# Seven block products in place of eight for most of w_down, one chunk of w_up later

## The chip, the cores and the metric

The kernel runs on one core of a Trainium2 chip. Its engines work side by side, each through its own queue in order: TensorE (PE, with its weight loads as PEld), VectorE (DVE), ScalarE (ACT), GpSimd (POOL) and SyncE (SP), which issues the loads and stores. The metric is the device time of one execution in microseconds, as the median of the runs; three runs of the kernel before gave 837.82 us (836.74 to 837.98).

## What is computed

One layer of a decoder: 512 tokens of 1024 features, fp32. Two token mixers come first (a convolution and an attention), then the channel mixer that the change touches, then a gated embedding and a final norm. In the reference the channel mixer reads:

```python
hf = rmsnorm(x, norm_ffn[i])
up = causal_dwconv(hf @ w_up[i], ffn_dw_w[i], ffn_dw_b[i])
gate, val = jnp.split(up, 2, axis=-1)
x = x + (jax.nn.gelu(gate) * val) @ w_down[i]
```

`w_up` is 1024 x 5632, `w_down` 2816 x 1024, and the convolution runs over three tokens.

## The kernel before

Matrix products run in two parts: each operand is cut into a hi part (ScalarE, `hi_of`, line 107) and a lo part (VectorE, `lo_of`, line 110: the operand less its hi part), and each product takes three matmuls: hi hi, hi lo and lo hi (`mm_w`, lines 117 to 119, with weights as the stationary operand; `mm_a`, lines 123 to 125, with activations as the stationary one).

Weights come as a stream of pieces (`pieces`, class `Stream`) in their order of use. A piece is 512 KB, 128 partitions by 1024 columns. `pump` asks for loads (two raw buffers, `wraw`) and starts cuts up to four cut pieces (`whl`) ahead; `take` hands a piece to its product; `done` frees it. So a cut stands some three pieces ahead of its use in the queues of ScalarE and VectorE.

The 2816 features of the channel mixer are 22 chunks of 128. For each chunk `up_chunk` runs twice, for the gate and for the value: 24 matmuls of 512 columns into one of the eight PSUM banks (`ps`), an eviction by ScalarE (line 1170) and two taps of the convolution by VectorE (lines 1171 and 1172). Then come the gelu (line 1180), the multiplication (line 1182) and the two parts `a` of the activations. After 8, 16 and 22 chunks `rows_product` multiplies the group by its rows of `w_down`: for each column half, four row tiles of tokens, accumulated over the group's chunks in four banks and then added to x in SBUF by VectorE (`residual`, line 1137). The third group goes on into the next norm.

The order of each queue is the order in which the program is written; what is moved by hand is where `pump` and `st.work` place the stages of a cut. SyncE's queue holds every load in the order of the pieces.

Of the kernel before, what the change touches and what calls it, by code (L numbers as in the profile page):

```python
# [11 lines left out]
F32R = mybir.dt.float32r  # L12
# [29 lines left out]
# heads whose scores, two units ahead, and whose weights, one unit ahead, are due in a unit's steps  # L42
# [41 lines left out]
def block_kernel(ctx: ExitStack, tc: tile.TileContext, x, p, rel_bias, norm_mix, w_in, conv_dw_w, conv_dw_b,  # L84
# [30 lines left out]
    # out += W.T a  with W's parts as the stationary operand  # L115
# [5 lines left out]
    # out += a.T W  with the activations' parts as the stationary operand  # L121
    def mm_a(o, a_hi, a_lo, w_hi, w_lo, start, stop):
        nc.tensor.matmul(o, a_hi, w_hi, start=start, stop=False)  # L123
        nc.tensor.matmul(o, a_hi, w_lo, start=False, stop=False)  # L124
        nc.tensor.matmul(o, a_lo, w_hi, start=False, stop=stop)  # L125

# [1 line left out]
    # A piece lands as fp32 and is cut into an exact (hi, lo) pair of float32r parts, some pieces ahead of its use.  # L128
# [24 lines left out]
    CMP_AFTER = CMP_AT                      # the compression's eight pieces follow the z pieces from this one on  # L153
# [10 lines left out]
    FFN_GROUPS = ((0, 8), (8, 16), (16, NF))  # L164
    for f0, f1 in FFN_GROUPS:
# [5 lines left out]
        rows_pieces("down%d" % f0, w_down, list(range(f0, f1)))  # L171
# [4 lines left out]
    class Stream:  # L176
# [6 lines left out]
        def pump(self, force=False):  # L183
            """asks for the next pieces; starts to cut those that were asked for in an earlier call"""
            while self.stages:
                self.work()
            while self.cuts < self.dmas and (force or self.asked[self.cuts] < self.call):
                i = self.cuts
                key, _, a, b, tag = pieces[i]
                if tag is not None:  # L190
                    if tag == "whl" and self.hls >= self.limit:
                        break
                    hl = work("whl", (P, 2, a, b), F32R, tag=tag, bufs=CUT if tag == "whl" else 1)
                    self.hl[i] = hl
                    self.cut(hl, self.raw[i], a)
                    self.hls += tag == "whl"
                    self.raws -= 1
                self.cuts += 1
            while self.dmas < len(pieces):
                i = self.dmas  # L200
                key, srcs, a, b, tag = pieces[i]
                if (self.wholes if tag is None else self.raws) == 2:
# [12 lines left out]

        def cut(self, hl, raw, a):
            """in stages, so that neither engine waits for the other"""
# [28 lines left out]

        def done(self):
            self.hls -= 1
# [3 lines left out]

    st = Stream()

# [13 lines left out]
    VNG = ((0, 3), (3, 3), (6, 2))          # row blocks of the values' and branch gates' weights  # L268
# [29 lines left out]
    for _ in range(WARM):                  # keeps the tensor engine's clock up until the first rows are there  # L298
        nc.tensor.matmul(warm[:, :P], ones, grow[:, 0:P], start=True, stop=True)
    nc.scalar.activation(sg[:, 0, 0:1], mhalf, AF.Sigmoid)  # L300

    class Norm:
        """RMS norm of one row tile, whose halves may come one after the other."""
# [32 lines left out]
        def to_T(self, hT, t):  # L336
            """-> hT[:, part, kc, tokens]"""
# [9 lines left out]
    def vec_rows(name, parts):  # L347
        """parts: list of [r, 128] APs stacked on partitions -> [128, sum r]."""
# [52 lines left out]
    # relative bias: W[q, h, j] = -bias_h(384 + q - j), +BIG where the distance is negative  # L401
# [7 lines left out]
    # the first tile's norm is shared out, as everything waits for it  # L409
# [75 lines left out]
    KQ = work("KQ", (P, 2, 2, NG, S), F32R, tag="B", bufs=2)   # [(dup d), branch, part, group, token]  # L485
    QQ = work("QQ", (P, NH, S), F32R, tag="B", bufs=2)         # [(part d), head, token]
# [48 lines left out]
    def kpe_evac(kv, o):  # L535
        """the windows' first (ab = 0) and second halves: k[s] + pe[16 ab + s % 16]"""
# [7 lines left out]
    def cmp_x(kv):  # L544
        """Xw[kv][ab][(r d), g, s] = kpe[(g d), s + r]"""
# [68 lines left out]
    def conv_steps():  # L614
        while len(conv_done) < 4 * (CONV_W - 1):
# [3 lines left out]
            # two chains take turns; an instruction then follows one that it doesn't wait for  # L619
# [9 lines left out]
    def conv_tail():  # L629
        """layer norm over channels (on transposed rows), then silu(x) = x/2 (1 + tanh(x/2))"""  # L630
# [103 lines left out]
    class Unit:  # L734
        """softmax weights of four heads (a group) over one branch's keys, for a tile of queries"""

        def __init__(self, t, g, b):
# [3 lines left out]
            per = min(HPG, 512 // self.nk)              # heads in a tile of 512  # L741
# [78 lines left out]
    def attention(order):  # L820
# [3 lines left out]
        def step(place, fn=None):  # L824
            """one step of the pipeline; fn is run a step later"""
# [7 lines left out]
        def ahead(i):  # L833
            """opens unit i"""
# [65 lines left out]
    class Pace:  # L900
        """runs steps of a generator at a rate, until it ends"""
# [142 lines left out]
    # per-layer embedding rows: p^T parts  # L1044
# [33 lines left out]

# [1 line left out]
    def rows_product(name, ks, a_of, done, late=None, filler=None, between=None, last=None):  # L1080
        """for every row tile t and column half n: done(t, n, psum of a.T @ w[:, half]);
        late(t): what follows a row tile's second half, on the tensor engine after the next tile's product."""
        for n in range(2):
            o = [ps() for _ in range(NT)]
# [61 lines left out]

    gain_f = load_gain(norm_ffn)
    hfT = work("hfT", (P, 2, KC, S), F32R, tag="A", bufs=1)
    hl_ple = st.take("ple", 0)
    for t in range(NT):  # L1150
# [4 lines left out]
                 lambda t: norms[t].to_T(hfT, t), lambda: ple_half(0, hl_ple))  # L1155

# [18 lines left out]
    hpT = gain_p = None  # L1175
    for f0, f1 in FFN_GROUPS:
        act = {}
        for f in range(f0, f1):
            ug = up_chunk(f)
            nc.scalar.activation(ug, ug, AF.Gelu_apprx_tanh)  # L1180
            uv = up_chunk(NF + f)
# [3 lines left out]
            lo_of(act[f][:, 1], uv, act[f][:, 0])  # L1185
        ks = list(range(f0, f1))
        a_of = lambda k, t: (act[k][:, 0, t * P:(t + 1) * P], act[k][:, 1, t * P:(t + 1) * P])
        if f1 < NF:
            rows_product("down%d" % f0, ks, a_of, lambda t, n, o: residual(t, n, o, None))
        else:  # L1190
            gain_p = load_gain(norm_ple)
            hpT = work("hpT", (P, 2, KC, S), F32R, tag="A", bufs=1)
            st.pump()
            hl_ple1 = st.take("ple", 1)
            rows_product("down%d" % f0, ks, a_of, lambda t, n, o: residual(t, n, o, gain_p),
                         lambda t: norms[t].to_T(hpT, t), lambda: ple_half(1, hl_ple1))

# [6 lines left out]
    def gate(t, c0, c1, o):  # L1204
        """x2 += sigmoid(o) * ple; ple holds half of it, and sigmoid(x) = (1 + tanh(x/2)) / 2"""
# [21 lines left out]
    def gate_last(hls, o):  # L1227
        """the last tile's second half in two parts, so that less follows the last product"""
# [55 lines left out]
```

## Time and profile before

| what | value |
|---|---|
| median of 3 runs | 837.82 us (836.74 to 837.98) |
| span of the profiled execution, first to last instruction | 835.6 us |
| TensorE busy | 821.3 us (98%) |
| VectorE busy | 539.6 us (65%) |
| ScalarE busy | 375.4 us (45%) |
| GpSimd busy | 24.7 us (3%) |
| granted TensorE clock, mean | 0.998 of full |

The profiled execution's own time is not listed beside its span, so the median less the span, 2.2 us, stands for what lies around it. The page lists each engine's busy time, a chain of work followed back from the last instruction, and groups of instructions by source line with their mean duration. A matmul's record is longer than the step from its start to the next one's start, so the steps tell TensorE's pace. Idle time of an engine that nobody waits for costs nothing.

### The profile page before, as it was taken

The page shows a single profiled execution, that of the slowest core. Times are in us where ns is not written, and L with a number is a line of the kernel's source. Part 1 is how long each engine was busy: PE and PEld are TensorE (multiplying, and loading weights), DVE is VectorE, ACT ScalarE, POOL GpSimd, SP SyncE. Part 2 cuts the span into 40 slices and gives each one's busy share as a digit, 9 for nine tenths or more (in the row PEclk, how much of TensorE's full clock was granted, in tenths as well). Part 3 has the DMA queues.
Part 4 walks back from the last instruction along what each step waited for, and adds up shares of the span by engine and source line. Part 5 has one row for each costly group of instructions (what it writes and reads, how often), then busy time and mean ns, then how long its engine had stood idle before and what let it go on. Part 6 is the DMA issues. An engine that isn't in the chain of part 4 may idle for free.

```text
span 835.6 us, 10144 instructions
## 1 busy us (share of the span) xinstructions
PE 821.3 (98%) x3872; PEld 669.0 (80%) x3872; DVE 539.6 (65%) x907; ACT 375.4 (45%) x677; POOL 24.7 (3%) x71
## 2 busy tenths in 40 slices
PE   7999999999999999999999999999999999999996
PEld 6888888888888886888788888888888888888885
DVE  6379977988987897935566663355654356655564
ACT  6332524287778874432544441234442123433443
POOL 2000000000010000001000000000000000001012
PEclk9999999999999999999999999999999999999999
DMA  7347787411110116430333324232333323341312
GB/s 217 83 112 202 165 188 173 96 51 51 51 51 27 51 52 219 134 101 26 100 101 102 93 85 125 80 94 81 99 100 102 101 75 102 102 147 55 120 32 101
DMA packets 108026, 84.54 MB, mean 101 GB/s; under 512 B 4080, under 2 KB 93608, under 8 KB 107978
## 3 DMA queue, kind: packets, MB, share of 16 engines
q1 hardware_dynamic: 107978, 83.90, 35.5%
q8 instruction: 30, 0.49, 0.3%
q14 instruction: 18, 0.15, 0.1%
HBM read 79.36 MB, written 2.43 MB: 98 GB/s over the span
## 4 chain that ended last, share of the span: by engine, by line
PE 96%; ACT 1%; DVE 1%; DMA 1%; issue 0%; POOL 0%; SPq 0%; POOLq 0%; ACTq 0%
PE ps L117 19%; PE ps L119 19%; PE ps L118 19%; PE ps L123 9%; PE ps L124 9%; PE ps L125 9%; PE ps L759 2%; PE ps L785 2%; PE ps L565 2%; PE ps L704 1%; PE ps L705 1%; PE ps L341 1%; PE ps L713 1%; DMA vraw<-in_w_in 1%; PE ps L803 0%
## 5 line engine op out<-in xcount | busy, mean ns | idle before, releaser
L110 DVE TENSOR_TENSOR whl<-wraw,whl 128x1024 fp32r<-128x1024 f32 (+1 forms) x159 | 155.6, 987 | 146.8 <-ACT whl L107 143.7
L107 ACT ACTIVATE whl<-wraw 128x1024 fp32r<-128x1024 f32 (+1 forms) x159 | 133.7, 862 | 124.2 <-PE ps L125 94.3
L117 PE MATMUL ps<-hfT,whl 128*128 128x512 f32 x352 | 139.1, 395 | 0.3 <-ACT hfT L107 0.3
L118 PE MATMUL ps<-hfT,whl 128*128 128x512 f32 x352 | 139.1, 395 | 0.2 <-DVE hfT L110 0.2
L119 PE MATMUL ps<-hfT,whl 128*128 128x512 f32 x352 | 139.0, 395 | 0.0
L117 PE MATMUL ps<-hT,whl 128*128 128x512 f32 x256 | 102.8, 402 | 0.0
L119 PE MATMUL ps<-hT,whl 128*128 128x512 f32 x256 | 101.1, 395 | 0.3 <-DVE whl L110 0.3
L118 PE MATMUL ps<-hT,whl 128*128 128x512 f32 x256 | 100.9, 394 | 0.0
L625 DVE SCALAR_TENSOR_TENSOR acc<-aT,convw,acc 128x512 f32<-128x512 f32 x120 | 86.2, 746 | 1.0
L118 PEld LDWEIGHTS ps<-hfT,whl 128*128 128x128 f32 x352 | 66.2, 188 | 16.4 <-DVE hfT L110 0.5
L117 PEld LDWEIGHTS ps<-hfT,whl 128*128 128x128 f32 x352 | 66.2, 188 | 16.2 <-ACT hfT L107 0.5
L119 PEld LDWEIGHTS ps<-hfT,whl 128*128 128x128 f32 x352 | 66.2, 188 | 15.9
L123 PE MATMUL ps<-whl,a 128*128 128x512 f32 x176 | 69.7, 396 | 0.0
L125 PE MATMUL ps<-whl,a 128*128 128x512 f32 x176 | 69.5, 395 | 0.0
L124 PE MATMUL ps<-whl,a 128*128 128x512 f32 x176 | 69.5, 395 | 0.0
L1170 ACT ACTIVATE up<-ps,ffnw 128x512 f32<-128x512 f32 x44 | 34.3, 780 | 61.5 <-PE ps L119 61.5
L1171 DVE SCALAR_TENSOR_TENSOR up<-ps,ffnw,up 128x511 f32<-128x511 f32 x44 | 33.0, 750 | 43.9 <-ACT up L1170 43.8
L119 PEld LDWEIGHTS ps<-hT,whl 128*128 128x128 f32 x256 | 48.2, 188 | 12.0 <-DVE whl L110 0.7
L117 PEld LDWEIGHTS ps<-hT,whl 128*128 128x128 f32 x256 | 48.2, 188 | 9.9 <-issue 0.2
L118 PEld LDWEIGHTS ps<-hT,whl 128*128 128x128 f32 x256 | 48.3, 189 | 9.4
L125 PEld LDWEIGHTS ps<-whl,a 128*128 128x128 f32 x176 | 33.0, 188 | 8.0
L123 PEld LDWEIGHTS ps<-whl,a 128*128 128x128 f32 x176 | 33.1, 188 | 7.9
(191 smaller groups left out, 1263.6 us busy)
## 6 DMA issues: line engine op xcount, KB each, us to landing
wraw<-in_w_up SPq DMA_DIRECT2D x44, 512.0 KB
wraw<-in_w_in SPq DMA_DIRECT2D x32, 512.0 KB
wraw<-in_w_down SPq DMA_DIRECT2D x22, 512.0 KB
wraw<-in_w_out SPq DMA_DIRECT2D x8, 512.0 KB
wraw<-in_w_ple_gate SPq DMA_DIRECT2D x8, 512.0 KB
W<-vdram SPq DMA_DIRECT2D x8, 264.0 KB
xin<-in_x SPq DMA_DIRECT2D x4, 512.0 KB
wraw<-in_w_ck SPq DMA_DIRECT2D x4, 512.0 KB
```

The costliest lines, as they stand in the source:

```text
L107: nc.scalar.activation(dst, src, AF.Copy, scale=scale)
L110: nc.vector.tensor_tensor(dst, src, f32(hi), op=ALU.subtract)
L117: nc.tensor.matmul(o, hl[:, 0, j, cs], a_hi, start=start, stop=False)
L118: nc.tensor.matmul(o, hl[:, 0, j, cs], a_lo, start=False, stop=False)
L119: nc.tensor.matmul(o, hl[:, 1, j, cs], a_hi, start=False, stop=stop)
L123: nc.tensor.matmul(o, a_hi, w_hi, start=start, stop=False)
L124: nc.tensor.matmul(o, a_hi, w_lo, start=False, stop=False)
L125: nc.tensor.matmul(o, a_lo, w_hi, start=False, stop=stop)
L565: nc.tensor.matmul(hid_ps[kv][hf], raw[:, jj, hf * P:(hf + 1) * P], Xw[kv][j // 8][:, :, s0:s0 + 16 * (NCMP - 1) + 1:16], start=j == 0, st ...
L625: nc.vector.scalar_tensor_tensor(acc[:, c, :], a[:, k:k + S], convw[:, 4 * k + c:4 * k + c + 1], acc[:, c, :], op0=ALU.mult, op1=ALU.add)
L1170: nc.scalar.activation(u, o, AF.Identity, scale=fw(2, c), bias=fw(3, c))
L1171: nc.vector.scalar_tensor_tensor(u[:, 1:], o[:, :S - 1], fw(1, c), u[:, 1:], op0=ALU.mult, op1=ALU.add)
```

## The change

The first 16 chunks now go in four groups of four. In a group the activations are a 2 x 2 matrix of blocks (first or second half of the tokens by even or odd chunk) and the rows of `w_down` another (even or odd chunk by column half). Their product is formed by seven block products of sums of blocks (the scheme of Strassen and Winograd) in place of eight. The sums of weight blocks (`Quad`, four subtractions of 1024 columns per group) and of activation blocks (`act_pair`, four of 256 columns per pair of chunks) run on GpSimd. A group's weights are loaded by four loads into one buffer `draw`; its seven operands (`11`, `t1`, `t2`, `21`, `t3`, `22`, `t4`) are cut like pieces. Two banks, `seeded`, are held through the whole stage: ScalarE copies the first product into them, and four products accumulate on top. A group's products are issued after the first chunk pair of the next group. The last group (chunks 16 to 21) stays as it was.

```diff
+    FFN_GROUPS = ((0, 4), (4, 8), (8, 12), (12, 16), (16, NF))
+    DOWN_OPS = ("11", "t1", "t2", "21", "t3", "22", "t4")
...
+            if f == f0 and g:
+                quad_pieces(FFN_GROUPS[g - 1][0])
...
+                if tag == "quad":
+                    quads[key[1]].sums()
+                elif tag == "op":
...
+                    self.cut(hl, quads[key[1]].at[key[2]], a)
+                    if key[2] == "11":
+                        self.stages.append(quads[key[1]].last_sum)
...
+    class Quad:
+        def __init__(self, f0):
+            raw = work("draw", (P, 4, 2, 512), tag="B", bufs=2)
...
+                nc.sync.dma_start(raw[:, i], rows[:, r, :, c * 512:(c + 1) * 512])
+        def sub(self, to, a, b):
+            nc.gpsimd.tensor_tensor(to, self.at[a], self.at[b], op=ALU.subtract)
+        def sums(self):
+            x = work("dsum", (P, 2, 2, 512), tag="accX")
+            self.at["t1"], self.at["t2"], self.at["t3"] = x[:, 0], x[:, 1], self.at["12"]
+            self.sub(x[:, 0], "12", "11")
+            self.sub(x[:, 1], "22", "t1")
+            self.sub(self.at["12"], "22", "12")
+        def last_sum(self):
+            self.at["t4"] = self.at["11"]
+            self.sub(self.at["11"], "21", "t2")
...
+    def act_pair():
+        raw = work("apair", (P, 2, 512), tag="pT", bufs=2)
+        for j in range(2):
+            uv = yield
+            nc.vector.tensor_tensor(raw[:, j], uv[0], uv[1], op=ALU.mult)
...
+        add = lambda to, a, b, op: nc.gpsimd.tensor_tensor(to, a, b, op=op)
+        add(s1, a21, a22, ALU.add)
+        add(s3, a11, a21, ALU.subtract)
+        add(s2, s1, a11, ALU.subtract)
+        add(s4, a12, s2, ALU.subtract)
...
+            hi_of(x_[:, 0], src)
+            lo_of(x_[:, 1], src, x_[:, 0])
...
+    def seven_products(f0, pairs):
...
+        m, e = [ps(), ps()], [ps(), ps()]
+        product(m, "11", "11", True)
+        for tt in range(2):
+            nc.scalar.activation(seeded[tt], m[tt], AF.Copy)
+        product(e, "s1", "t1", True)
+        product(seeded, "s2", "t2", False)
+        add_to(1, 1, e)
+        add_to(0, 1, seeded)
+        product(m, "12", "21", False)
+        add_to(0, 0, m)
+        product(seeded, "s3", "t3", False)
+        add_to(1, 1, seeded)
+        product(e, "s4", "22", False)
+        add_to(0, 1, e)
+        product(seeded, "22", "t4", False)
+        add_to(1, 0, seeded)
...
         for f in range(f0, f1):
-            ug = up_chunk(f)
-            nc.scalar.activation(ug, ug, AF.Gelu_apprx_tanh)
-            uv = up_chunk(NF + f)
+            ug, uv = up_pair(f)
+            if waiting:
+                st.skip("quad", waiting[0])
+                seven_products(*waiting)
+                waiting = None
```

VectorE's queue around a group's `w_down` product, before: the last chunk's taps and multiplication, then cuts (`whl`) and adds into x (line 1137) in blocks.

```order
L1172 SCALAR_TENSOR_TENSOR up<-ps,ffnw_816,up 128x510
L1182 TENSOR_TENSOR up<-up 128x512
L110 TENSOR_TENSOR a<-up,a 128x512
L110 TENSOR_TENSOR whl<-wraw,whl 128x1024 x4
L1137 TENSOR_TENSOR x_3159<-ps,x_3159 128x512 x4
L110 TENSOR_TENSOR whl<-wraw,whl 128x1024 x4
L1137 TENSOR_TENSOR x_3159<-ps,x_3159 128x512 x4
```

And now, around the seven products (line 1267 is the add into x, `draw` and `dsum` hold weight blocks and their sums):

```order
L110 TENSOR_TENSOR whl<-dsum,whl 128x1024
L1231 SCALAR_TENSOR_TENSOR up<-ps,ffnw_816,up 128x511
L1232 SCALAR_TENSOR_TENSOR up<-ps,ffnw_816,up 128x510
L110 TENSOR_TENSOR whl<-draw,whl 128x1024 x3
L1267 TENSOR_TENSOR x_3159<-ps,x_3159 128x512 x4
L110 TENSOR_TENSOR whl<-draw,whl 128x1024
L1267 TENSOR_TENSOR x_3159<-ps,x_3159 128x512 x2
L110 TENSOR_TENSOR whl<-wraw,whl 128x1024
L1267 TENSOR_TENSOR x_3159<-ps,x_3159 128x512 x2
L110 TENSOR_TENSOR whl<-wraw,whl 128x1024
L1267 TENSOR_TENSOR x_3159<-ps,x_3159 128x512 x2
L110 TENSOR_TENSOR whl<-wraw,whl 128x1024
```

Twelve adds stand between seven cuts where eight stood between eight, in a stretch that feeds 84 matmuls where 192 were fed.

ScalarE's queue ahead of a group's products, before: eviction, gelu, the hi part of `a`, and a run of nine cuts.

```order
L1170 ACTIVATE up<-ps,ffnw_820 128x512
L1180 ACTIVATE up<-up 128x512
L107 ACTIVATE whl<-wraw 128x1024
L1170 ACTIVATE up<-ps,ffnw_820 128x512
L107 ACTIVATE a<-up 128x512
L107 ACTIVATE whl<-wraw 128x1024 x9
```

And now, from the second pair's activations to the copies into the seeded banks (line 1283):

```order
L107 ACTIVATE a<-apair 128x512
L107 ACTIVATE a<-apair 128x256
L107 ACTIVATE a<-asums 128x512 x2
L107 ACTIVATE whl<-dsum 128x1024
L1230 ACTIVATE up<-ps,ffnw_820 128x512
L1299 ACTIVATE up<-up 128x512
L107 ACTIVATE whl<-dsum 128x1024
L1230 ACTIVATE up<-ps,ffnw_820 128x512
L107 ACTIVATE whl<-draw 128x1024
L1283 ACTIVATE ps<-ps 128x512 x2
L107 ACTIVATE whl<-draw 128x1024 x3
```

The hi parts of the sums and the cuts of t1 and t2 (`dsum`) read what GpSimd writes, and the next chunk's evictions stand behind them.

GpSimd's queue had nothing in the channel mixer; a group now has, from its first pair's sums to the last weight sum:

```order
L1246 TENSOR_TENSOR asums<-apair 128x256 x2
L1246 TENSOR_TENSOR asums<-asums,apair 128x256
L1246 TENSOR_TENSOR asums<-apair,asums 128x256
L297 TENSOR_TENSOR dsum<-draw 128x1024
L297 TENSOR_TENSOR dsum<-draw,dsum 128x1024
L297 TENSOR_TENSOR draw<-draw 128x1024
L1246 TENSOR_TENSOR asums<-apair 128x256 x2
L1246 TENSOR_TENSOR asums<-asums,apair 128x256
L1246 TENSOR_TENSOR asums<-apair,asums 128x256
L297 TENSOR_TENSOR draw<-draw,dsum 128x1024
```

The sums t1, t2 and t3 stand ahead of the second pair's sums, and t4 behind them.

## Rows read from the trace of the kernel before

**Rows 1.** The page: busy time of each engine; the chain's shares by engine.

```profile
PE 821.3 (98%) x3872; PEld 669.0 (80%) x3872; DVE 539.6 (65%) x907; ACT 375.4 (45%) x677; POOL 24.7 (3%) x71
...
PE 96%; ACT 1%; DVE 1%; DMA 1%; issue 0%; POOL 0%; SPq 0%; POOLq 0%; ACTq 0%
```

**Rows 2.** Waits of TensorE, 400 to 790 us: total, times, longest.

```profile
PE ps L117 <- ACT hfT L107: 0.3, 1, 0.3
PE ps L118 <- DVE hfT L110: 0.2, 1, 0.2
```

**Rows 3.** Timeline of TensorE in a w_down product: start, duration, instruction.

```profile
494.02 0.40 PE L123 MATMUL ps<-whl,a 128*128 128x512 f32 x1
...
503.81 0.40 PE L123 MATMUL ps<-whl,a 128*128 128x512 f32 x1
```

**Rows 4.** Busy us of each engine in stretches of the mixer, and their sum.

```profile
404.90:494.00 89.10, 89.08 (x383) 72.27 (x384) 53.38 (x62) 38.30 (x48) 0.00 (x0) 1.00 0.33 95
494.00:538.00 44.00, 44.00 (x190) 35.41 (x189) 16.86 (x19) 9.78 (x10) 0.00 (x0) 1.00 0.33 101
...
sum 380.10, PE 380.08 PEld 306.98 DVE 206.01 ACT 142.45 POOL 3.83; mean PE 63.35 PEld 51.16 DVE 34.34 ACT 23.74 POOL 0.64
```

**Rows 5.** Groups by line, VectorE and ScalarE: count | busy, mean ns | idle before.

```profile
L110 DVE TENSOR_TENSOR whl<-wraw,whl 128x1024 fp32r<-128x1024 f32 x89 | 108.6, 1224 | 126.4 <-ACT whl L107 126.1
L1171 DVE SCALAR_TENSOR_TENSOR up<-ps,ffnw,up 128x511 f32<-128x511 f32 x44 | 33.0, 750 | 43.9 <-ACT up L1170 43.8
L1137 DVE TENSOR_TENSOR x<-ps,x 128x512 f32<-128x512 f32 x32 | 21.5, 687 | 13.8 <-PE ps L125 13.8
L110 DVE TENSOR_TENSOR a<-up,a 128x512 fp32r<-128x512 f32 x22 | 15.2, 693 | 15.4 <-ACT a L107 15.4
...
L107 ACT ACTIVATE whl<-wraw 128x1024 fp32r<-128x1024 f32 x89 | 93.3, 1052 | 99.7 <-PE ps L125 94.3 <-DMA wraw<-in_w_in 4.0 <-DMA wraw<-in_w_down 1.0
L1170 ACT ACTIVATE up<-ps,ffnw 128x512 f32<-128x512 f32 x44 | 34.3, 780 | 61.5 <-PE ps L119 61.5
L107 ACT ACTIVATE a<-up 128x512 fp32r<-128x512 f32 x22 | 13.9, 632 | 51.3 <-DVE up L1182 51.3
L1133 ACT ACTIVATE ple<-ps 128x512 f32<-128x512 f32 x8 | 4.5, 603 | 1.9 <-PE ps L125 1.9
```

**Rows 6.** Groups of GpSimd by line, in the same columns.

```profile
L327 POOL TENSOR_TENSOR rstd<-ss 128x1 f32<-128x1 f32 x16 | 5.7, 353 | 54.1 <-ACT junk L314 53.4 <-ACT junk L1242 0.7
L510 POOL MEMSET VC<- 32x256 f32 x1 | 0.3, 303 | 0.0
L1267 POOL MEMSET const-float32-0.0<- 128x1 f32 x1 | 0.1, 98 | 0.2 <-issue 0.2
```

**Rows 7.** Timeline of GpSimd alone, and beside VectorE's rows.

```profile
371.39 0.21 POOL L318 TENSOR_SCALAR ss<-ss 128x1 f32<-128x1 f32 x1 [0.39 <-ACT junk L314]
385.29 0.19 POOL L327 TENSOR_TENSOR rstd<-ss 128x1 f32<-128x1 f32 x1 [4.67 <-ACT junk L314]
...
807.79 2.86 POOL L318 TENSOR_SCALAR ss<-ss 128x1 f32<-128x1 f32 x4 [27.30 <-ACT junk L314]
808.70 2.49 DVE L1250 TENSOR_TENSOR x<-x,gain 128x512 f32<-128x512 f32 x4
...
829.92 0.69 DVE L1221 TENSOR_TENSOR x<-x,gain 128x512 f32<-128x512 f32 x1 [0.63 <-ACT junk L1242]
830.03 0.63 POOL L327 TENSOR_TENSOR rstd<-ss 128x1 f32<-128x1 f32 x1 [0.67 <-ACT junk L1242]
```

**Rows 8.** Timeline near 241 us, and the group of VectorE's row.

```profile
240.81 0.57 POOL L660 TENSOR_TENSOR brs<-brs,mhalf 128x1 f32<-128x1 f32 x1
241.07 0.16 DVE L774 TENSOR_TENSOR ar<-ar,sg 128x4 f32<-128x4 f32 x1
...
L774 DVE TENSOR_TENSOR ar<-ar,sg 128x4 f32<-128x4 f32 x16 | 2.6, 165 | 0.6
```

**Rows 9.** Stretch with four queued loads: busy by engine, clock, DMA share, GB/s.

```profile
326.00:328.00 2.00, 1.02 (x4) 0.86 (x5) 2.00 (x4) 1.22 (x2) 0.00 (x0) 1.00 1.00 398
```

More of the change, by code (lines that the diff above doesn't have):

```diff
@@ L245, in take, with skip @@
             return self.hl[i] if pieces[i][4] is not None else self.raw[i]
+        def skip(self, *key):
+            assert pieces[self.taken][0] == key
+            self.taken += 1
         def done(self):
@@ L1077, in block_kernel, with rows_product @@
             nc.vector.scalar_tensor_tensor(yT[m][:, 1], ysum[m], 0.5, f32(yT[m][:, 0]), op0=ALU.mult, op1=ALU.subtract)
-    def rows_product(name, ks, a_of, done, late=None, filler=None, between=None, last=None):
+    def rows_product(name, ks, a_of, done, late=None, filler=None, between=None, last=None, banks=None):
         for n in range(2):
-            o = [ps() for _ in range(NT)]
+            o = [banks[t] if n and banks and t < len(banks) else ps() for t in range(NT)]
             def part(t, kk, hl):
@@ L1145, in residual @@
             norms[t].rows()
+    seeded = [ps(), ps()]
     gain_f = load_gain(norm_ffn)
@@ L1154, in block_kernel @@
                  lambda t, n, o: residual(t, n, o, gain_f),
-                 lambda t: norms[t].to_T(hfT, t), lambda: ple_half(0, hl_ple))
+                 lambda t: norms[t].to_T(hfT, t), lambda: ple_half(0, hl_ple), banks=seeded)
     def fw(k, c):
@@ L1173, in up_chunk @@
         return u
-    hpT = gain_p = None
+    def act_pair():
[3 more added lines that the diff above has]
+            nc.vector.tensor_tensor(raw[:, j], uv[0], uv[1], op=ALU.mult)
+        sums = [work("asums", (P, 2, 256), tag="S", bufs=8) for _ in range(2)]
+        a11, a21, a12, a22 = (raw[:, j, h * 256:(h + 1) * 256] for j in range(2) for h in range(2))
+        s1, s3, s2, s4 = sums[0][:, 0], sums[0][:, 1], sums[1][:, 0], sums[1][:, 1]
+        add = lambda to, a, b, op: nc.gpsimd.tensor_tensor(to, a, b, op=op)
[3 more added lines that the diff above has]
+        add(s4, a12, s2, ALU.subtract)
+        parts = {}
+        for src, names in ((raw[:, :, 0:256], ("11", "12")), (a22.unsqueeze(1), ("22",)), (sums[0], ("s1", "s3")),
+                           (sums[1], ("s2", "s4"))):
+            n = len(names)
+            x_ = work("a", (P, 2, n, 256), F32R, tag="act", bufs=8)
+            hi_of(x_[:, 0], src)
+            lo_of(x_[:, 1], src, x_[:, 0])
+            for i, name in enumerate(names):
+                parts[name] = x_[:, :, i]
+        yield parts
@@ new lines, in seven_products, with add_to, product @@
+    def seven_products(f0, pairs):
+        x_ = lambda r, c, tt: x2[:, 2 * r + tt, c * 512:(c + 1) * 512]
+        def add_to(r, c, bank):
+            for tt in range(2):
+                nc.vector.tensor_tensor(x_(r, c, tt), bank[tt], x_(r, c, tt), op=ALU.add)
+        def product(bank, a, b, start):
+            st.pump()
+            hl = st.take("down", f0, b)
+            for tt in range(2):
+                ts = slice(tt * P, (tt + 1) * P)
+                for i, pair in enumerate(pairs):
+                    mm_a(bank[tt], pair[a][:, 0, ts], pair[a][:, 1, ts], hl[:, 0, i, :], hl[:, 1, i, :],
+                         start and i == 0, i == len(pairs) - 1, skip_group_check=True)
+                st.work()
+            st.done()
+        m, e = [ps(), ps()], [ps(), ps()]
+        product(m, "11", "11", True)
+        for tt in range(2):
+            nc.scalar.activation(seeded[tt], m[tt], AF.Copy)
[11 more added lines that the diff above has]
+        add_to(1, 0, seeded)
@@ L1176, in block_kernel, with up_pair @@
+    def up_pair(f):
+        ug = up_chunk(f)
+        nc.scalar.activation(ug, ug, AF.Gelu_apprx_tanh)
+        return ug, up_chunk(NF + f)
+    hpT = gain_p = waiting = None
     for f0, f1 in FFN_GROUPS:
-        act = {}
+        act, pairs = {}, []
         for f in range(f0, f1):
-            ug = up_chunk(f)
-            nc.scalar.activation(ug, ug, AF.Gelu_apprx_tanh)
-            uv = up_chunk(NF + f)
+            ug, uv = up_pair(f)
[3 more added lines that the diff above has]
+                waiting = None
+            if f1 < NF:
+                if (f - f0) % 2 == 0:
+                    pair = act_pair()
+                    next(pair)
+                parts = pair.send((ug, uv))
+                if parts:
+                    pairs.append(parts)
+                continue
@@ L1185, in block_kernel @@
             lo_of(act[f][:, 1], uv, act[f][:, 0])
+        if f1 < NF:
+            waiting = f0, pairs
+            continue
         ks = list(range(f0, f1))
         a_of = lambda k, t: (act[k][:, 0, t * P:(t + 1) * P], act[k][:, 1, t * P:(t + 1) * P])
[L1188 to L1196, printed above, removed]
+        gain_p = load_gain(norm_ple)
+        hpT = work("hpT", (P, 2, KC, S), F32R, tag="A", bufs=1)
+        st.pump()
+        hl_ple1 = st.take("ple", 1)
+        rows_product("down%d" % f0, ks, a_of, lambda t, n, o: residual(t, n, o, gain_p),
+                     lambda t: norms[t].to_T(hpT, t), lambda: ple_half(1, hl_ple1))
     gain_o = load_gain(norm_final)
```

35 lines of the change are left out of this document (27 added, 8 removed).

## The prediction

> **What bounds the kernel now.** I read the page's totals first, then the chain, then what TensorE waited for in the channel mixer, then the engines that serve it. TensorE is busy 98% of 835.6 us and 96% of the chain that ended last is TensorE [rows 1]. From 400 to 790 us, the channel mixer, it waited 0.5 us in all, for its first activations [rows 2]. Its instructions follow each other at a fixed step: from the `w_down` matmul that starts at 494.02 to the one at 503.81 there are 42 steps, 9.79 / 42 = 0.233 us each [rows 3]. So in this stretch time is the number of matmuls times 0.233 us, as long as every operand is there in time. The other engines have room on average: in 89.1 us of `w_up` products VectorE is busy 53.4 (60%) and ScalarE 38.3, in 44 us of `w_down` products VectorE 16.9 (38%), GpSimd nothing [rows 4].
>
> **What the change removes.** One group of four chunks of `w_down` took 4 chunks x 4 row tiles x 2 column halves x 3 parts = 96 matmuls; now it is 7 products x 2 row tiles x 2 chunk pairs x 3 parts = 84, of the same shape (128x128 by 512 columns). Four groups: 48 matmuls fewer, 48 x 0.233 = 11.2 us off the path, if the step stays [rows 3]. The profiled execution's span is 835.6 us and the median of the runs is 837.82 us; I take the 2.2 us between them as fixed.
>
> **What it adds.** Per group, with durations from the groups of lines [rows 5]:
> - ScalarE: three more weight cuts (7 operands in place of 4 pieces), 3 x 1.05; two copies of a bank into the seeded banks, nearest row the 0.60 us eviction of `ple` from PSUM; the activations' hi parts in 3 x 0.63 + 0.4 per pair where 2 x 0.63 were. Together some 6.5 us per group, 26 us in all.
> - VectorE: three more cuts, 3 x 1.22; twelve adds into x at 0.69 where a group of eight chunks took eight, so four; lo parts 3 x 0.69 + 0.42 per pair in place of 2 x 0.69. Together 3.7 + 5.5 + 2.2 = 11.4 us per group, 45 us in all.
> - GpSimd, which did nothing here: four subtractions of 1024 columns and eight of 256 per group.
> - SyncE: a group's weights come as four loads of 512 KB in a burst, some 24 us ahead of the first product. With four loads queued the queue moved 398 GB/s [rows 9], so 2 MB take 5.3 us; the loads hide.
>
> None of it is TensorE's. VectorE goes from 206 us of 380 [rows 4] to some 251 of 369, so on average it still fits. What decides is whether it fits at the one place where the work is dense: a group's seven products, 7 x 12 x 0.233 = 19.6 us, in which no `w_up` chunk gives it rest.
>
> **The dense place, laid out.** I put the order's rows end to end with the durations of [rows 5], each starting when its engine's previous row and its operands are done, 0.05 us per handover; time 0 is the first product's start, and the products start at 0, 2.8, 5.6, 8.4, 11.2, 14.0 and 16.8. The group's last `w_up` chunk ends at -11.2 (one pair of chunks earlier: this is what the move later buys). Eviction 0.78, two taps 2 x 0.75 and the multiplication (0.69, as a lo part) bring the pair's activations at -7.8. Four sums, each 0.7 us on GpSimd (below), end at -4.9, and their hi and lo parts at -3.5. The cut of t1 ends at -2.0 and is due at 2.8. Next on ScalarE come two evictions, the gelu (0.63, as a hi part), the cuts of t2 and 21 and the copies, done at 3.8 and due at 5.6. On VectorE then stand three cuts and four adds, done at 10.6, and the product of s3, which writes into the seeded banks that these adds read, is due at 11.2. The next adds are done at 15.3 and due at 16.8. So TensorE waits nowhere, but the margins are 4.8, 1.8, 0.6 and 1.4 us. For the smallest I charge 0.1 us per group, 0.4 in all.
>
> **GpSimd's price, which no row shows.** Its widest row here is a fill: 303 ns for 256 columns against 98 ns for one, that is 0.8 ns a column; its two-input rows have one column and take 0.19 us alone [rows 7] and 353 ns on the mean [rows 6]. A fill writes only. One pass at this rate bounds a 1024-column subtraction below at 0.9 us; two reads and a write one after the other give 2.6. I take 2.2, nearer the upper end, as both inputs have to be read; 0.7 for 256 columns. The Trainium skill (GPSIMD Engine Reference, section 3.1) has 4497 ns for an add of 2048 columns, by which 1024 columns would be an estimated 2.25 us and the sum would not move. Up to 3.2 us the layout keeps its zero, if GpSimd hinders nobody.
>
> **Does it hinder VectorE?** In one direction the trace answers. A one-column GpSimd addition takes 0.19 us alone, but 0.63 us when VectorE runs a `tensor_tensor` with both inputs in SBUF: VectorE's row ends at 829.92 + 0.69 = 830.61, GpSimd's at 830.66; and four that took 0.21 alone took 2.86 beside such rows [rows 7]. GpSimd waits for a VectorE instruction of two SBUF inputs; the weight cuts, the lo parts and the multiplication are of this kind, the taps and adds (one input in PSUM) are not. In the other direction there is one row: from 240.81 to 241.38 GpSimd runs a two-input instruction, and VectorE's two-input row at 241.07 takes 0.16 us inside it, its usual 165 ns [rows 8]. VectorE was not held. It is weak, since the GpSimd row had one column to read. I forecast by it: GpSimd is stretched, VectorE is not. Stretched by a cut or two, a subtraction takes 2.2 + 1 = 3.2 us and the layout loses 0 to 1.2 us per group, at the products of t2 and s3.
>
> **Forecast:** 837.8 - 11.2 + 0.4 = 827.0 us, alone 825.5 to 832 (4 x 1.2 us lost at the upper end).
>
> **Rival 1, slower: the two engines exclude each other both ways.** If a running subtraction also holds VectorE's two-input rows, the place is the 20 us from t1's sum to the cut of t1. There VectorE has two multiplications, two cuts and four lo parts (0.69 + 1.22 + 1.22 + 0.69 + 2.5), four taps (3.0) and the cut of t1 (1.22), 10.5 us; GpSimd has four subtractions and four sums, 4 x 2.2 + 4 x 0.7 = 11.6 us; handovers 0.8; two taps run beside GpSimd (less 1.5 to 3.0). That is 20.6 against 19.8: t1's product starts 0.8 late. From the cut of t1 on, taps 1.5, gelu 0.63, cut of t2 1.04, eviction 0.78, cut of 21 1.04 and a copy follow in turn, 5.3 us where t1's product lasts 2.8: 2.5 more. The adds before s3 cost 0.4. Sum 3.7 per group, 14.7 in all: 837.8 - 11.2 + 14.7 = 841.3. By the same count 2.0 us per subtraction cost 10.1 (836.7, no change) and 2.4 cost 19.4 (846.0); the rival turns slower above some 2.1 us. For it: the chip plainly gives that read path to one engine at a time [rows 7]. Against it: [rows 8]. The Trainium skill (SBUF — State Buffer, "Who interferes with whom") states this rule: an instruction of either engine takes the shared pair for its whole length and the other blocks. The trace agrees in VectorE's favour and shows no case in GpSimd's; by the page the time is that of this rival.
>
> **Rival 2: GpSimd is just slower,** with nobody excluded. The sums then come late to ScalarE, whose queue holds the next evictions and cuts behind them. By the same layout 3.6 us for 1024 columns lose 1.0 us per group (837.8 - 11.2 + 4.0 = 830.6), and 4.0 us lose 3.0, which takes the whole saving (838.5). Against it: the rate of [rows 6].
>
> **Rival 3: the products don't keep the step.** 28 of them each change to banks that another engine has just read or written. A drain (a matmul lasts 0.40, its step 0.233 [rows 3]) and a handover cost 0.2 to 0.4 us each, 6 to 11 us in all: 832 to 838, the saving gone. Against it: changes of bank between `w_up` chunks cost nothing before [rows 2].
>
> **How the numbers follow.** Forecast 0.44; rival 1 0.45 (0.35 slower, 0.06 no change, 0.04 faster, as a subtraction takes over 2.1, about 2.0 or under 1.9 us); rival 2 0.05 (0.03 faster, 0.01, 0.01); rival 3 0.06 (0.02 faster, 0.01, 0.03). Faster by over 0.2%, about what runs of this kernel can tell apart: 0.44 + 0.04 + 0.03 + 0.02 = 0.53; within it 0.08; slower 0.39. Rival 1 taken whole is as likely as the forecast, but its time is spread over 830 to 850, so the predicted time stays 827.0. The range is 825 to 846: it leaves out rival 1 with subtractions over 2.4 us (some 0.12) and the tails.
>
> **What will show it.** Right: the mixer's matmuls at 0.233 us with under 0.5 us of waiting per group; cuts of 1024 columns still 1.22 us while GpSimd runs; GpSimd's 1024-column rows at 2 to 3.5 us. Rival 1: cuts and lo parts that end with a GpSimd row or start late after it, and TensorE idle before t1's and t2's products. Rival 2: ScalarE waiting for GpSimd's sums, cuts at their old length. Rival 3: a gap before every product. The forecast is wrong above all if a subtraction takes VectorE's second input for its whole length.

## The result, and the profile after

The kernel with seven products takes 833.16 us (median; 831.23 to 833.77) where the one before takes 837.72: 4.6 us less, a ratio of 0.9944 with a 95% interval of 0.9930 to 0.9958. So it is faster, but by less than half of the 10.8 us that were forecast. The page's first line answers to [rows 1]:

```profile
PE 812.2 (98%) x3824; PEld 660.7 (79%) x3824; DVE 595.5 (72%) x967; ACT 397.5 (48%) x713; POOL 97.6 (12%) x119
```

TensorE has its 48 matmuls fewer (3872 to 3824). What it waited for in the channel mixer, in total, times and longest, answers to [rows 2]:

```profile
PE ps L123 <- ACT ps L1283: 4.5, 4, 2.0
```

This row is new, beside the two of [rows 2], which are unchanged: four waits, one per group, for ScalarE's copies of the first product into the seeded banks (line 1283). The timeline of TensorE in the first group shows where; the first product starts at 461.26, and the rows are the ends and starts of the products of t1, t2, 21 and t3:

```profile
466.63 0.40 PE L125 MATMUL ps<-whl,a 128*128 128x512 f32 x1
467.70 0.50 PE L123 MATMUL ps<-whl,a 128*128 128x512 f32 x1 [0.67 <-ACT ps L1283]
468.04 0.39 PE L124 MATMUL ps<-whl,a 128*128 128x512 f32 x1
...
473.15 0.39 PE L125 MATMUL ps<-whl,a 128*128 128x512 f32 x1
473.60 0.48 PE L123 MATMUL ps<-whl,a 128*128 128x512 f32 x1
473.92 0.40 PE L124 MATMUL ps<-whl,a 128*128 128x512 f32 x1
```

Two steps that should be 0.233 us [rows 3] take 1.07 and 0.34 before t2's product: 0.94 us lost. Before t3's product they take 0.45 and 0.32: 0.30 lost, with no wait named. Counted so, the four groups lose 0.94, 1.33, 1.05 and 2.24 us at t2's product and 0.30, 0.27, 0.27 and 0.29 at t3's, 6.7 in all. No other step of the products is over 0.26. The saving was 11.2; 11.2 - 6.7 = 4.5, which is the whole result. So the question is what makes the copies late.

Excerpts of the timelines of GpSimd, VectorE and ScalarE in the 24 us ahead of it (start, duration, instruction, and in brackets idle time and what ended it):

```profile
445.42 2.52 POOL L297 TENSOR_TENSOR dsum<-draw 128x1024 f32<-128x1024 f32 x1 [10.30 <-DMA draw<-in_w_down]
448.01 2.41 POOL L297 TENSOR_TENSOR dsum<-draw,dsum 128x1024 f32<-128x1024 f32 x1
450.37 3.40 POOL L297 TENSOR_TENSOR draw<-draw 128x1024 f32<-128x1024 f32 x1
454.46 0.74 POOL L1246 TENSOR_TENSOR asums<-apair 128x256 f32<-128x256 f32 x1 [0.69 <-DVE apair L1242]
455.16 1.19 POOL L1246 TENSOR_TENSOR asums<-apair 128x256 f32<-128x256 f32 x1
456.31 0.92 POOL L1246 TENSOR_TENSOR asums<-asums,apair 128x256 f32<-128x256 f32 x1
457.31 1.07 POOL L1246 TENSOR_TENSOR asums<-apair,asums 128x256 f32<-128x256 f32 x1
458.34 2.40 POOL L297 TENSOR_TENSOR draw<-draw,dsum 128x1024 f32<-128x1024 f32 x1
```

```profile
448.82 2.68 DVE L110 TENSOR_TENSOR whl<-draw,whl 128x1024 fp32r<-128x1024 f32 x1 [1.71 <-ACT whl L107]
451.42 0.74 DVE L1231 SCALAR_TENSOR_TENSOR up<-ps,ffnw,up 128x511 f32<-128x511 f32 x1
452.98 1.34 DVE L1242 TENSOR_TENSOR apair<-up 128x512 f32<-128x512 f32 x1
455.02 0.73 DVE L110 TENSOR_TENSOR a<-apair,a 128x512 fp32r<-128x512 f32 x1 [0.70 <-ACT a L107]
455.67 0.95 DVE L110 TENSOR_TENSOR a<-apair,a 128x256 fp32r<-128x256 f32 x1
457.05 0.73 DVE L110 TENSOR_TENSOR a<-asums,a 128x512 fp32r<-128x512 f32 x1 [0.42 <-ACT a L107]
459.08 2.21 DVE L110 TENSOR_TENSOR a<-asums,a 128x512 fp32r<-128x512 f32 x1 [1.30 <-ACT a L107]
461.22 1.21 DVE L110 TENSOR_TENSOR whl<-dsum,whl 128x1024 fp32r<-128x1024 f32 x1
```

```profile
463.97 0.63 ACT L1299 ACTIVATE up<-up 128x512 f32<-128x512 f32 x1 [3.30 <-DVE up L1232]
464.50 1.05 ACT L107 ACTIVATE whl<-dsum 128x1024 fp32r<-128x1024 f32 x1
465.46 0.76 ACT L1230 ACTIVATE up<-ps,ffnw 128x512 f32<-128x512 f32 x1
466.12 1.05 ACT L107 ACTIVATE whl<-draw 128x1024 fp32r<-128x1024 f32 x1
467.06 1.07 ACT L1283 ACTIVATE ps<-ps 128x512 f32<-128x512 f32 x2
```

VectorE's rows of two SBUF inputs end a fixed time after the GpSimd row that they met: their records have begun, but most of their work comes after its end. I call such a row held. GpSimd's row at 448.01 ends at 450.42; VectorE's cut, begun at 448.82, ends 1.08 later and so takes 2.68 in place of 1.22 [rows 5]. GpSimd's next row, begun at 450.37, in turn takes 3.40 in place of 2.40, the 1.0 us more being the cut. It ends at 453.77, and the multiplication, begun at 452.98, ends 0.55 later: 1.34 in place of 0.69. t4's subtraction ends at 460.74, and the last lo part, begun at 459.08, ends 0.55 later: 2.21 in place of 0.69. The 256-column sums do the same on a smaller scale. The first takes 0.74; the lo part at 455.02 ends 0.55 after it, and the second sum, which met that lo part, ends 0.60 after the lo part's end and so takes 1.19. The 256-column lo part at 455.67 ends 0.28 after the second sum, 0.95 in place of 0.42. So four sums that would take 4 x 0.74 = 2.96 us take 3.92. The tap at 451.42, one input in PSUM, keeps its 0.74 inside a GpSimd row. So the two engines exclude each other in both directions. The Trainium skill (SBUF — State Buffer, "Who interferes with whom") states this rule; here the trace agrees with it, with these numbers, at 256 and at 1024 columns ([rows 8] stays an exception, see the last section).

From the lo part on it is one chain: t1's cut, two taps, gelu, cut of t2, eviction, cut of 21 and the two copies until 468.13. The first of them ends at 467.65 and was due at 466.9 (5.6 after 461.26); t2's product starts at 467.70.

### The profile page after: what moved, and what is told of

Same layout as the page of the kernel before. It is cut to its first block, busy times and chain, and to the rows that moved or that the text cites. A ratio compares the mean times of both kernels' runs of the same rounds, so it can differ in the third digit from the quotient of the medians.

```text
span 831.2 us, 10240 instructions
## 1 busy us (share of the span) xinstructions
PE 812.2 (98%) x3824; PEld 660.7 (79%) x3824; DVE 595.5 (72%) x967; ACT 397.5 (48%) x713; POOL 97.6 (12%) x119
## 5 line engine op out<-in xcount | busy, mean ns | idle before, releaser
L110 DVE TENSOR_TENSOR whl<-wraw,whl 128x1024 fp32r<-128x1024 f32 (+1 forms) x143 | 135.8, 959 | 88.5 <-ACT whl L107 88.1
L107 ACT ACTIVATE whl<-wraw 128x1024 fp32r<-128x1024 f32 (+1 forms) x143 | 117.1, 842 | 94.1 <-PE ps L125 42.7
L118 PEld LDWEIGHTS ps<-hfT,whl 128*128 128x128 f32 x352 | 66.3, 188 | 16.2 <-DVE hfT L110 0.5
L123 PE MATMUL ps<-whl,a 128*128 128x512 f32 x160 | 64.0, 400 | 4.7 <-ACT ps L1283 4.5
L125 PE MATMUL ps<-whl,a 128*128 128x512 f32 x160 | 63.2, 395 | 0.0
L124 PE MATMUL ps<-whl,a 128*128 128x512 f32 x160 | 63.1, 395 | 0.0
L123 PEld LDWEIGHTS ps<-whl,a 128*128 128x128 f32 x160 | 30.1, 188 | 14.7 <-ACT ps L1283 6.3
L824 ACT ACTIVATE S<-S,am 128x512 f32<-128x512 f32 (+3 forms) x64 | 35.3, 554 | 5.1 <-DVE am L819 4.8
```

The lines of the kernel that those rows point to most:

```text
L107: nc.scalar.activation(dst, src, AF.Copy, scale=scale)
L110: nc.vector.tensor_tensor(dst, src, f32(hi), op=ALU.subtract)
L118: nc.tensor.matmul(o, hl[:, 0, j, cs], a_lo, start=False, stop=False)
L123: nc.tensor.matmul(o, a_hi, w_hi, start=start, stop=False, **kw)
L124: nc.tensor.matmul(o, a_hi, w_lo, start=False, stop=False, **kw)
L125: nc.tensor.matmul(o, a_lo, w_hi, start=False, stop=stop, **kw)
```

## The experiments

Theory A is this exclusion. Theory B is that the copies stand too far back in ScalarE's queue, whoever computes the sums. Theory C is rival 3, a gap of its own wherever a product changes banks.

Each ratio below is to runs of the kernel before taken beside the run (medians 837.66 and 837.47).

**Without the weight sums.** The operands are blocks as they are, without the subtractions (an excerpt):

```diff
-            self.sub(x[:, 0], "12", "11")
-            self.sub(x[:, 1], "22", "t1")
-            self.sub(self.at["12"], "22", "12")
+            self.at["t1"], self.at["t2"], self.at["t3"] = self.at["12"], self.at["22"], self.at["12"]
...
-            self.sub(self.at["11"], "21", "t2")
```

> The four sums of weight blocks per group are left out (t1, t3 take block 12, t2 block 22, t4 block 11 as they are, so the output is not the reference's); the activation sums stay on GpSimd, everything else as in the changed kernel. Theory A: GpSimd's 1024-column subtractions and VectorE's two-input rows exclude each other both ways, and this makes the copies into the seeded banks late. It expects no VectorE row of 2.2 us or more in the mixer, TensorE's waits for the copies down from 4.5 us to under 0.3, the 0.2 us gap at s3 gone, and 826 to 827.5 us. Theory B: the copies are late because they stand on ScalarE behind two evictions, a gelu and two cuts, whoever runs the sums. It expects 4 us of waits still and 832 to 833.5 us. Theory C: a gap wherever a product changes to banks that another engine has just written, 0.9 us or more at s2 and 0.2 at s3 in each group: also 832 to 833.5.

Measured: 826.57 us (826.05 to 827.86; ratio to before 0.987, 0.9853 to 0.9888). TensorE waits for nothing in the products and no step is over 0.26 us. VectorE's lo parts of the activation sums (durations least, median, most), in the changed kernel and then here:

```profile
L110 DVE TENSOR_TENSOR a<-asums,a x16: 691/733/2223, 433.8 to 657.0; 128x512 fp32r<-128x512 f32 x16
```

```profile
L110 DVE TENSOR_TENSOR a<-asums,a x16: 692/713/734, 432.8 to 650.3; 128x512 fp32r<-128x512 f32 x16
```

The 2.2 us rows are gone, with the order of ScalarE's and TensorE's queues as it was. The copies in the first group (line 1278 here):

```profile
464.03 1.06 ACT L1278 ACTIVATE ps<-ps 128x512 f32<-128x512 f32 x2
```

They end 4.70 us after the first product's start (460.39), as in the other three groups, where the changed kernel has 6.87, 7.24, 6.96 and 8.14. B and C fall as causes by themselves. Nor was it a sum that came late: in the changed kernel t1's and t2's sums had ended by 450.42, and ScalarE began to cut them at 458.95 and 464.50. The activation sums, still on GpSimd, make TensorE wait for nothing when they are alone there.

**t4's sum a little later.** It is the subtraction at 458.34 above, and its result is first read at 470.85, by ScalarE's cut of t4, 10 us after the subtraction's end. Written into t1's buffer, it can't start before t1's cut has read t1:

```diff
-                    if key[2] == "11":
+                    if key[2] == "t1":
                         self.stages.append(quads[key[1]].last_sum)
...
-            self.at["t4"] = self.at["11"]
-            self.sub(self.at["11"], "21", "t2")
+            self.at["t4"] = self.at["t1"]
+            self.sub(self.at["t1"], "21", "t2")
```

> t4's sum is written into t1's buffer in place of 11's, so that it can't start before t1's cut has been read; its place in the program is one cut later. The sums are the same. Theory A: the lo part of s2 and s4, held until 2.2 us by t4's subtraction, takes 0.75 again; the cut of t1, the gelu, the cut of t2, the cut of 21 and the copies come 1.5 us earlier; waits for the copies are 0 in three groups and under 0.6 in the fourth, 827 to 829 us. Theories B and C: unchanged, 832 to 833.5.

Measured: 827.79 us (827.45 to 828.62; ratio 0.9884, 0.9868 to 0.9900). VectorE's last lo part and t1's cut, the first tap behind, GpSimd's subtraction, and all that TensorE still waited for:

```profile
458.66 0.69 DVE L110 TENSOR_TENSOR a<-asums,a 128x512 fp32r<-128x512 f32 x1 [1.29 <-ACT a L107]
459.62 1.23 DVE L110 TENSOR_TENSOR whl<-dsum,whl 128x1024 fp32r<-128x1024 f32 x1 [0.26 <-ACT whl L107]
460.76 0.74 DVE L1231 SCALAR_TENSOR_TENSOR up<-ps,ffnw,up 128x511 f32<-128x511 f32 x1
```

```profile
460.92 2.40 POOL L297 TENSOR_TENSOR dsum<-draw,dsum 128x1024 f32<-128x1024 f32 x1 [2.96 <-DVE whl L110]
```

```profile
PE ps L123 <- ACT ps L1283: 0.6, 1, 0.6
```

The same 2.40 us now lie beside the two taps and idle time of VectorE, and cost nothing. The lo part takes 0.69 again; in three groups no step is lost, at t3's product neither. The one wait left is in the fourth group. There GpSimd's first subtraction, which waits for its load, starts 14.5 us ahead of the first product (16.2 in the first group), and the multiplication meets the start of a subtraction (2.74 us for 0.69). One subtraction's place was worth 5.4 us.

**t4's sum twice**, a dose of the same:

```diff
             self.sub(self.at["11"], "21", "t2")
+            self.sub(self.at["11"], "21", "t2")
```

> t4's subtraction is issued twice in a row (same result), one more GpSimd instruction of 2.4 us per group, and nobody needs it before the last product, 16 us later. Theory A: it holds the lo part or the cut of t1 behind it by another 2.4 us, and the copies with them: 4 x 2.4 = 9.6 us more, 841 to 844 us. Theories B and C: GpSimd has room, so 832.5 to 834.

Measured: 843.85 us (843.29 to 846.46; ratio 1.0081, 1.0059 to 1.0102), slower than before the change. GpSimd's two rows, VectorE's cut of t1, and TensorE's waits:

```profile
457.60 5.21 POOL L297 TENSOR_TENSOR draw<-draw,dsum 128x1024 f32<-128x1024 f32 x2
```

```profile
460.48 3.42 DVE L110 TENSOR_TENSOR whl<-dsum,whl 128x1024 fp32r<-128x1024 f32 x1
```

```profile
PE ps L123 <- ACT ps L1284: 8.0, 4, 2.4
PE ps L124 <- DVE whl L110: 3.2, 4, 2.1
```

The second subtraction started before the cut of t1, which was held as the lo part had been: 3.42 in place of 1.22, per group. Now t1's product waits too, as rival 1 had it (the copies are line 1284 here). An instruction that nobody waits for moved the end by 10.7 us against the changed kernel. That this meets the 9.6 us of theory A is in part luck: by the steps the products lose 18.6 us in place of 6.7, 11.9 more, and some 4.6 of these are matmuls at half the clock in three groups (last section); the first product starts 0.75 us earlier here, so the end moves by less. The holds by themselves cost some 7 us.

**One input in place of two.** GpSimd copies the first operand:

```diff
-            nc.gpsimd.tensor_tensor(to, self.at[a], self.at[b], op=ALU.subtract)
+            nc.gpsimd.tensor_copy(to, self.at[a])
```

> Each of GpSimd's 1024-column weight subtractions becomes a copy of its first operand, one input in place of two (the sums are left out, so the output is not the reference's). It asks what it is that excludes. Theory A in the form that only instructions of two inputs on both sides exclude each other: cuts beside a copy keep 1.22 us, and the time is that of the kernel without weight sums, 826 to 827.5. Theory A in the form that any long GpSimd instruction holds VectorE's two-input rows: the cut of 11 and the last lo part are stretched by what is left of the copy, and the time lies between 827.5 and 833. Theories B and C: 832 to 833.5.

Measured: 826.88 us (826.69 to 827.05; ratio 0.9873, 0.9855 to 0.9890), no waits. The time is that of the first form of the theory, but the rows say the second. In the fourth group, GpSimd's copy and VectorE's cut of 11:

```profile
641.33 1.04 POOL L297 COPY draw<-draw 128x1024 f32<-128x1024 f32 x1
```

```profile
641.56 1.88 DVE L110 TENSOR_TENSOR whl<-draw,whl 128x1024 fp32r<-128x1024 f32 x1 [1.71 <-ACT whl L107]
```

The copy ends at 642.37, the cut 1.07 later, the same distance as beside a subtraction. So a one-input copy holds VectorE too. It costs TensorE no time: the copy lasts 1.04 us where the subtraction lasts 2.40, and elsewhere it holds VectorE's rows only at its end (the last lo part takes 0.83 at most).

**The copies earlier.** ScalarE's queue alone: the cut of 21 behind the copies in place of ahead of them (an excerpt of `product` and of what follows the first one):

```diff
-            st.pump()
+            if b != "11":
+                st.pump()
             hl = st.take("down", f0, b)
...
             nc.scalar.activation(seeded[tt], m[tt], AF.Copy)
+        st.pump()
```

> Only ScalarE's order is changed: the two copies into the seeded banks stand before the cut of 21 in place of behind it; all sums stay where they are. If the lateness of the copies is a chain in which each microsecond counts alike, whether it comes from the exclusion or from the queue, the copies come 1.04 us earlier, TensorE's losses at s2 of 0.95, 1.34, 1.06 and 2.25 us become 0, 0.3, 0 and 1.2, and the time is 829 to 830.5 us. If the exclusion alone decides, 832 to 833.5.

Measured: 832.48 us (832.22 to 833.13; ratio 0.9941, 0.9927 to 0.9955), not distinguishable from the changed kernel. The time lies in the second range, but not by its reasoning: the copies did come earlier (465.90 in the first group, 4.8 us after the first product's start, where the changed kernel has 5.8), but the wait moved. TensorE's waits, and VectorE's rows in the first group:

```profile
PE ps L123 <- DVE x L1267: 4.1, 4, 1.0
PE ps L123 <- ACT ps L1284: 1.1, 1, 1.1
```

```profile
467.97 3.50 DVE L110 TENSOR_TENSOR whl<-draw,whl 128x1024 fp32r<-128x1024 f32 x3
471.38 2.48 DVE L1267 TENSOR_TENSOR x<-ps,x 128x512 f32<-128x512 f32 x4
```

t3's product now waits 1.0 us for the adds that free the seeded banks. VectorE is as late as ScalarE, from the same holds: its three cuts start 6.90 us after the first product's start, against 6.91 in the changed kernel. There the wait at t2's product had covered this second lateness down to 0.3 us. So each of the two queues alone is late enough to cost most of it, and the cause lies ahead of both.

**All sums on VectorE.**

```diff
-            nc.gpsimd.tensor_tensor(to, self.at[a], self.at[b], op=ALU.subtract)
+            nc.vector.tensor_tensor(to, self.at[a], self.at[b], op=ALU.subtract)
...
-        add = lambda to, a, b, op: nc.gpsimd.tensor_tensor(to, a, b, op=op)
+        add = lambda to, a, b, op: nc.vector.tensor_tensor(to, a, b, op=op)
```

> All sums, of weight blocks and of activations, run on VectorE in place of GpSimd, at the same places of the program. By the exclusion theory a GpSimd subtraction costs VectorE up to 2.4 us while its own would cost 1.2 us, so VectorE loses nothing by doing the work itself: t1's sums now wait in VectorE's queue for their load, with the taps behind them, about 1 us; the chain to the copies is 0.5 to 2 us shorter than now; 828 to 832 us. If GpSimd's sums were mostly hidden (they run beside taps and idle time), VectorE gets 33 us of work on top and the dense place is late: 834 us or more.

Measured: 827.24 us (826.75 to 827.79; ratio 0.9877, 0.9864 to 0.9891). VectorE's sums, and the page's first line:

```profile
443.43 1.23 DVE L297 TENSOR_TENSOR dsum<-draw 128x1024 f32<-128x1024 f32 x1 [0.55 <-DMA draw<-in_w_down]
...
455.55 0.42 DVE L1246 TENSOR_TENSOR asums<-asums,apair 128x256 f32<-128x256 f32 x1
```

```profile
PE 811.4 (98%) x3824; PEld 660.5 (80%) x3824; DVE 603.7 (73%) x1015; ACT 396.8 (48%) x713; POOL 24.8 (3%) x71
```

VectorE does a weight sum in 1.23 us and an activation sum in 0.42, where GpSimd takes 2.40 and 0.74 or more. By these rows it took over 4 x 4 x 1.23 + 8 x 4 x 0.42 = 33 us of work, but its busy time rose by 8.2 us only (595.5 to 603.7): in the changed kernel the multiplications (line 1242) had taken 15.2 us where 16 x 0.69 is 11.0, the cuts of `draw` 28.8 for 20 x 1.22 = 24.4, and the lo parts of the activations 30.4 for 19.9. These 19 us of holding are gone; the rest of the difference, some 6 us, is not taken apart here (records of rows that follow directly overlap by some 0.08 us, which busy time counts once). No wait of TensorE is named, but in the fourth group four steps at t2's and t3's products still lose 0.6 us.

**t4's sum late, activation sums on VectorE** (the second edit above with the second line of the last one).

> t4's sum late, as in the run with t4's sum in t1's buffer, and the activation sums on VectorE (about 0.4 us each in place of 0.92 and 1.07 on GpSimd, which also stand in turn with ScalarE's and VectorE's parts). The chain from the multiplication to the copies should be some 2 us shorter again: no wait and no gap in any group, 826 to 827.3 us, the time of the kernel without weight sums. If VectorE's added 1.6 us per pair comes back elsewhere, 827.5 to 829.

Measured: 826.93 us (826.30 to 827.64; ratio 0.9874, 0.9860 to 0.9887), no wait and no longer step in any of the four groups. It has the lowest median with all the sums in it, though not distinguishable from the last one, and within 0.4 us of the kernel without weight sums.

**No delay.** The products directly behind their own group:

```diff
-            if f == f0 and g:
-                quad_pieces(FFN_GROUPS[g - 1][0])
+        if f1 < NF:
+            quad_pieces(f0)
...
-            waiting = f0, pairs
+            st.skip("quad", f0)
+            seven_products(f0, pairs)
             continue
```

> The products of a group directly behind its last chunk, in place of one chunk of w_up later; the weight operands one chunk earlier too. The eviction, taps, multiplication, sums and parts of the last pair, about 9 us before s1 is there, have no matmuls beside them. Both theories expect TensorE idle before the first product (eviction 0.78, taps 1.5, multiplication 0.7, parts 0.9: about 4 us) and before t1's (four sums, two more parts: 1 to 4 us): 5 to 8 us per group, 850 to 866 us. If the delay was not needed, 833.

Measured: 860.09 us (859.46 to 861.04; ratio 1.027, 1.0256 to 1.0284). TensorE's first `w_down` row that waits in the first group, and the stretches around it (busy time of each engine, then the granted clock):

```profile
456.76 0.79 PE L123 MATMUL ps<-whl,a 128*128 128x512 f32 x1 [6.26 <-ACT a L107]
```

```profile
450.30:456.70 6.40, 0.20 (x1) 0.00 (x0) 3.98 (x5) 2.86 (x5) 0.57 (x1) 0.72 0.01 1
456.70:459.90 3.20, 3.13 (x7) 2.44 (x8) 2.29 (x3) 0.95 (x3) 3.12 (x4) 0.50 0.00 0
```

The wait is 6.2 to 6.3 us in each group. It stands inside the first product, after three matmuls, where the second pair's activations come in, and not, as expected, in part before t1's; the total is inside the expected range, its split is not as expected. After it TensorE runs eight to fifteen matmuls at half its clock (1.2 of 2.4 GHz). By the steps 6.4 us are lost at the gap and 1.6 to 2.9 behind it, 33.8 in the four groups; less 11.2 this is 22.6, which is what the run takes more than the kernel before beside it (837.47). The delay by one chunk is worth 27 us; without it the seven products lose.

## Why the prediction was right and wrong

**Right: the saving and its price list.** 48 matmuls at 0.233 us were saved; the version with all sums in which no step is lost takes 826.9 us, where the forecast was 827.0. TensorE never waited for a load of `w_down` in the products, though GpSimd's first subtraction did; and the work added on ScalarE cost nothing where VectorE was in time. A 1024-column subtraction takes 2.40 us where I took 2.2 between 0.9 and 2.6, and a 256-column sum that is not held 0.74 where I took 0.7.

**Wrong: "GpSimd is stretched, VectorE is not".** This is the step that failed. I took [rows 8] for the direction that no other row showed, while saying that its GpSimd row has one column to read. The runs show VectorE held in every group, and the 0.4 us that the sum charged for the dense place was 6.7. Placed on the forecast's time scale, with the first product at 0, the first group went so: the sums end at -2.9 (forecast -4.9), the activation parts at 0.0 (-3.5), t1's cut at 1.2 (-2.0), the copies at 6.9 (3.8, due 5.6). The 3.1 us are the multiplication held 0.65, the last lo part held 1.5, and four sums that take 3.9 for 2.9 because VectorE's lo parts stand between them: I had stretched the subtractions alone. Without the two holds the copies would have been done at 4.7, in time, and 4.70 is where the run without weight sums has them. The margin of 1.8 us at the copies was thus the one that broke, and the one of 0.6 at t3's product followed.

**Right mechanism, wrong size: rival 1.** At 2.4 us per subtraction it gave a loss of 19.4 us and 846.0; the loss was 6.7. (Its terms as they are written, with the subtraction alone changed, add up to 18.0 at 2.4 us and 11.6 at 2.0, not 19.4 and 10.1.) The term that was mis-sized is the place from t1's sum to the cut of t1, 20.6 us at 2.2 and so 21.4 at 2.4; it took 445.42 to 462.43, 17.0 us. t1's product was then not late but 1.6 us early. Three things in the rows explain most of it. GpSimd started at -15.8 where I had it at -17.0, on the landing of its load, and by then one of the two multiplications and one of the two cuts were done (443.85 and 444.46: 1.9 us). All four taps ran beside it, not two. And the rows did take turns, but at each change some 0.14 us of the waiting row were already done (0.55 for 0.69, 1.08 for 1.22): the four sums and the three lo parts among them, 2.96 + 1.80 us end to end, took 3.92. Behind the cut of t1 the rival was right: 5.3 us until a copy is done by its count (5.6 if its terms are added up), 5.2 by the rows.

**Rivals 2 and 3.** GpSimd at 2.40 us is below the 3.2 at which rival 2 began; the ScalarE waits for GpSimd's sums are there, and harmless without the holds. Rival 3 falls: in three versions (without weight sums, with copies on GpSimd, and with t4's sum late and the activation sums on VectorE) all 28 products follow each other without a gap.

**The time** lies inside the range of 825 to 846, which spans the forecast and most of rival 1, and outside the forecast's own 825.5 to 832.

## What to carry to other kernels

Work given to GpSimd isn't free: here a GpSimd row of 256 or 1024 columns that reads SBUF cost VectorE's two-input rows nearly all the time that they overlapped, so count it as VectorE's work unless it lies beside rows with an input in PSUM, or idle time. Look for the instruction that is issued early and needed late: a subtraction that nobody waited for cost 5.4 us through the queue that it held, and a buffer dependence put it where it was free. When an edit removes a wait and the time stays, look where the wait has gone before giving up the theory.

## What the runs showed of the hardware that was not expected

- A held row ends a fixed time after the row that held it. VectorE's rows end 0.28, 0.55 and 1.08 us after it at 256, 512 and 1024 columns, where they last 0.42, 0.69 and 1.22 alone; GpSimd's end 0.60 and 2.27 after it at 256 and 1024, where they last 0.74 and 2.40. So the hold lasts until the other row's end, and some 0.14 us of the held row are done before it.
- A GpSimd sum costs (2.40 - 0.74) / 768 = 2.16 ns per column, with some 0.19 us that are not per column.
- [rows 8] stays unexplained: GpSimd's one-column power of 0.57 us holds nobody, and VectorE's row inside it takes 0.16 to 0.17 us in every trace of this case. No run here tells what sets it apart.
- A GpSimd copy of 1024 columns takes 1.04 us, less than half of a subtraction.
- TensorE's clock fell to half (1.2 of 2.4 GHz) after short waits in the run with t4's sum twice. In the first group a wait of 2.39 us ended at 469.17, and from about 470.5 the clock was 0.50 of full for 3.3 us; in the fourth, 2.1 us of waiting were followed by 0.51 for 3.5 us. In the third group a wait of 2.38 us was followed by the full clock. The stretches of the first, fourth and third group:

```profile
470.50:473.80 3.30, 3.30 (x9) 2.61 (x8) 3.30 (x5) 1.07 (x3) 0.00 (x0) 0.50 0.00 0
671.70:675.20 3.50, 3.48 (x8) 2.81 (x9) 1.76 (x3) 2.00 (x3) 0.00 (x0) 0.51 0.00 0
```

```profile
607.50:609.00 1.50, 1.50 (x7) 1.24 (x8) 1.50 (x2) 1.50 (x3) 0.00 (x0) 1.00 0.00 0
```

So the length of one wait alone doesn't tell whether the clock falls. Where it did, the slow steps cost 1.5 us in each of three groups of this run, and 1.5 to 2.8 us in the groups of the run without delay.
